# An RWKV layer's chain outputs in two tiles by steps, its inverse issued as one block, and mid products on 64 rows

## The chip, the cores and the metric

One core of a Trainium2 chip runs the whole program. The metric is the device time in microseconds, the median of three runs before. TensorE is PE in the rows, VectorE is DVE, ScalarE is ACT, GpSimd is POOL, SyncE is SP; PEld is TensorE's loading of weights.

## What is computed

Two blocks of a network on a sequence of 512 tokens of width 1024, in float32: attention and an MLP, an RWKV-7 mixer and an MLP, then a second block with a state space model, a linear recurrent unit and a gate. The change is in the RWKV mixer alone. It has 16 heads of 64 and two directions; per direction:

```
def rwkv7_scan(r, w, k, v, kk, a):
    def step(state, inp):
        r_t, w_t, k_t, v_t, kk_t, a_t = inp
        sa = jnp.einsum('bhvk,bhk->bhv', state, -kk_t)
        state = (state * w_t[:, :, None, :] + sa[..., None] * (kk_t * a_t)[:, :, None, :]
                 + v_t[..., None] * k_t[:, :, None, :])
        return state, jnp.einsum('bhvk,bhk->bhv', state, r_t)
...
        o = rwkv7_scan(*ins)
        if d == 1:
            o = jnp.flip(o, axis=1)
        bonus = jnp.sum(rh * kd * r_k.astype(F32), axis=-1, keepdims=True) * vh
        dir_out.append((group_norm(o, gn_w, gn_b) + bonus.reshape(nB, S, D)) * g.astype(F32))
```

The group norm is over the 64 outputs of a head at a token.

## The kernel before

The mixer takes heads in eight pairs (`p` from 0 to 7) and the 512 tokens in eight chunks of 64. In place of a scan over tokens it solves each chunk with small matrices and carries a 64 by 64 state from chunk to chunk. Both directions run at once: step `n` of the chain works on chunk `n` of direction 0 and on chunk `7 - n` of direction 1 (`chunk_of`). Direction 0 and direction 1 (or the two heads of a pair) sit in the two halves of the 128 partitions; `H(i)` is half `i`, `Q(i)` a quarter.

The work of a pair is written as eleven generators, and each is repeated over the pairs (line 1983):

- `values` (line 1526) projects the values once for all pairs; as it ends it frees its pools and opens others (`late`).
- `front` (1558) loads keys and norms them (products with `sel`, then transposes in `head_bcast`, line 1516); `half` (1595), once per direction, makes decays and the scaled keys `bk` and `ar`.
- `scores` (1677) makes for each of four chunk pairs the masked score matrices in a tile `at` and stores their diagonal blocks (`nd_s`). There are nine `at` tiles, so line 1681 lets a chunk pair's scores start only when the chain has freed the one nine before.
- `inverse` (1713) loads the blocks of 16 by 16 into `X` and, by way of `XL`, in transposed form, and inverts them by elimination in 28 VectorE steps; `merge` (1760) loads them back (`yd`), transposes them (`zd`) and puts them together into inverses of chunks, `tt`.
- `early` (1738) makes the values `uv`.
- `mid` (1830) makes for each chunk pair the matrix `m` that takes the state over a chunk, and the rest of `uv`. Its products `ahead` are issued one chunk pair ahead; then come products of `ax` with `tt`, ScalarE's copies into `ta` and `uv`, products of `at` with `ta`, and VectorE's adds into `m`.
- `chain` (1892) runs the eight steps: products of `uv` with `at` (`free`, begun with zeros from `zb` so that the later ones add), of the state `ss` with `m`, ScalarE's four copies into the next state, and two copies of outputs into `o`.
- `post` (1932) squares and sums `o`, takes the power -1/2 on GpSimd, scales, transposes, adds weights and bonus, multiplies by the gate and stores `y_s`.

What sets the order of all this is `weave` (line 37). It runs the generators beside each other. At each `yield` a generator names the engine and the tiles that its next instructions need, or gives a condition that must hold first. `weave` keeps an account of when each engine and tile would be free by its own costs, resumes the generator that could start first, and fixes each engine's order so. A generator that yields less often is issued in longer blocks. Products go into five banks of PSUM (`pm`, the tile `mb`) that are taken in turn, the chain's into three others (`cp`).

The conditions that the change touches are these two:

```
                    yield lambda: done["post"] > p - 1 and late      # line 1894, chain
                    yield lambda: done["step"] >= 8 * p + 8          # line 1949, post
```

With them `o` is one tile, written by eight steps of a pair and then normed as a whole. After the layer's last `post` the output projection loads `y_s` (line 1997) and the rest of the program follows.

Of the kernel before, what the change touches and what calls it, by code (L numbers as in the profile page):

```python
# [13 lines left out]
ALU = mybir.AluOpType  # L14
# [10 lines left out]
class Net:  # L25
# [1279 lines left out]
    def rwkv(self, g_pre, mu_p, mu_n, w_r, w_k, w_v, w_o, k_k, k_a, r_k, gn_w, gn_b, w0, w1, w2, a0, a1, a2,  # L1305
# [64 lines left out]
        with c0:  # L1370
# [86 lines left out]
            with ExitStack() as c1:  # L1457
# [19 lines left out]
                tts, ss, tas = zeros("tt", [8, 2, 64]), zeros("ss", [2, 128]), zeros("ta", [2, 2, 2, 64])  # L1477
                for j, t in enumerate(tts + ss + tas):
                    (V, G)[j % 2].memset(t, 0.0)
# [15 lines left out]
                done["side", 0] = done["side", 1] = 0  # L1495
# [217 lines left out]
                def inverse(p, st):  # L1713

                    yield lambda: done["pre"] > p
                    XL = sh.tile([128, 16, 32], F32, name="XL", tag="v1")
# [9 lines left out]
                    for j in range(1, 15):  # L1726
# [11 lines left out]
                def early(p, st):  # L1738
# [91 lines left out]
                def mid(p, st):  # L1830
# [5 lines left out]
                    def ahead(i):  # L1836
                        b = bank().rearrange("p (j h e x) -> p j h e x", j=2, h=2, e=2)
                        at = st["q", i]
                        for j in range(2):
# [3 lines left out]
                            for hp in range(2):  # L1843
                                for d in range(2):
                                    MM(b[H(d), j, hp, 1, :], at[:, j, hp, 2 * d, H(d)], uv[d][:, cs[d], hp, :], True, True)
                        return b

                    for i in range(4):
# [33 lines left out]
                        for d in range(2):  # L1882
                            cs = slice(6 - 2 * i, 8 - 2 * i) if d else slice(2 * i, 2 * i + 2)
                            r = ar[d][:, cs, 1 - d, :]
                            TT(V, m[:, :, d, H(d)], b[:, :, d, H(d)], r[:, ::-1] if d else r, AD)
                        i4 = lambda t: t.rearrange("p j d x -> p j (d x)")[:, :, 64:192].rearrange("p j (d x) -> p j d x", d=2)
                        TT(V, i4(m), i4(b), ident2.unsqueeze(1).unsqueeze(1).to_broadcast([128, 2, 2, 64]), AD)
# [4 lines left out]
                def chain(p, st):  # L1892

                    yield lambda: done["post"] > p - 1 and late
                    o = late["o"].tile([128, 8, 2, 64], F32, name="o", tag="o")
                    st["o"] = o
# [11 lines left out]
                    for n in range(8):  # L1908
                        if n % 2 == 0:
# [17 lines left out]
                        for d in range(2):  # L1927
                            ACT(o[H(d), chunk_of(n)[d]].rearrange("p h v -> p (h v)"), cp[H(d), d, :], AF.Copy)
# [3 lines left out]
                def post(p, st):  # L1932
# [14 lines left out]
                    yield lambda: done["step"] >= 8 * p + 8  # L1947
                    o = st["o"]
                    o3 = o.rearrange("p c h v -> p (c h) v")
                    rn = stp.tile([128, 16], F32, name="rg", tag="rg")  # L1950
                    for hf in range(2):
                        sq = TQ().rearrange("p (a b) -> p a b", b=64)
                        yield AC, o
                        ACT(sq, o3[:, 8 * hf:8 * hf + 8], AF.Square)
                        yield DV, sq
                        V.tensor_reduce(out=rn[:, 8 * hf:8 * hf + 8], in_=sq, axis=AX.X, op=AD)
                    yield DV, rn
                    TS(V, rn, rn, 1.0 / 64, 64e-5, M, AD)
                    yield PO, rn
# [198 lines left out]
```

## Time and profile before

| | us |
|---|---|
| runs (3): median, lowest, highest | 2320.56, 2318.47, 2324.29 |
| the profiled execution's own time | 2327.65 |
| its span, first to last instruction | 2325.9 |
| TensorE busy in the span | 2139.8 (92%) |
| VectorE, ScalarE, GpSimd busy | 1276.5 (55%), 1084.3 (47%), 91.3 (4%) |
| mean granted TensorE clock | 0.950 of full speed |

The profile page gives the busy time of each engine, forty equal slices of the span, the DMA queues, the chain that ended last and the costliest groups of instructions. The helpers `TT`, `STT`, `ACT` and `MM` record nearly all of the mixer's instructions under lines 1312, 1313, 1315 and 1316, so a row is told apart by the tiles that it names, written as out<-in. A float32 product stands in the trace as two instructions. Busy time counts an instruction from start to its modelled end.

### The profile page before, as it was taken

Reading aid. Unit: us, or ns where it says so; the run is one execution under the profiler, and the core shown is the slowest. Engines: PE = TensorE matmul, PEld = TensorE weight load, DVE = VectorE, ACT = ScalarE, POOL = GpSimd, SP = SyncE. Lnnn points to the kernel's source line nnn. Section 1 sums busy time; section 2 is a strip of 40 time slices with the busy share of each in tenths; the row PEclk is TensorE's granted clock in tenths of the full one; section 3 lists DMA queues with packets and bytes.
Section 4 is the critical chain, followed back from the end, with each engine's and each line's share of the span. In section 5 each row is a group of like instructions: output and inputs, shape, how many; then the busy total and the mean of one; then the engine's idle time right before and its main releaser. Section 6 shows DMA issues by size and latency. Waiting matters only on the chain. (4 is left out here: it accounts for less than half of the span.)

```text
span 2325.9 us, 40409 instructions
## 1 busy us (share of the span) xinstructions
PE 2139.8 (92%) x16330; PEld 1725.7 (74%) x16330; DVE 1276.5 (55%) x2597; ACT 1084.3 (47%) x1982; POOL 91.3 (4%) x123
## 2 busy tenths in 40 slices
PE   8998999999978788888888789999999999999998
PEld 6777788888866566666666568887788877788877
DVE  4656542333488765666764264387645567633353
ACT  4555353332366554777766545333233444522332
POOL 0000000000000001111100000000001000000000
PEclk9999999999989888899999799999999988899999
DMA  5311233233333233222222243334334544233341
GB/s 173 105 55 54 71 95 100 76 114 91 91 103 96 93 102 78 63 57 57 53 55 47 103 127 116 91 91 143 111 112 142 149 120 119 56 94 89 106 145 55
DMA packets 320902, 221.02 MB, mean 95 GB/s; under 512 B 82406, under 2 KB 274442, under 8 KB 320714
## 3 DMA queue, kind: packets, MB, share of 16 engines
q1 hardware_dynamic: 319418, 213.70, 32.3%
q10 hardware_dynamic: 1296, 4.72, 0.6%
q8 instruction: 129, 2.11, 0.4%
q14 instruction: 59, 0.48, 0.1%
HBM read 187.10 MB, written 27.07 MB: 92 GB/s over the span
## 5 line engine op out<-in xcount | busy, mean ns | idle before, releaser
L161 ACT ACTIVATE whi<-raw 128x1024 fp32r<-128x1024 f32 x220 | 231.2, 1053 | 534.8 <-PE mm L234 288.0
L162 DVE TENSOR_TENSOR wlo<-raw,whi 128x1024 fp32r<-128x1024 f32 x220 | 266.3, 1214 | 363.5 <-ACT whi L161 361.3
L233 PE MATMUL mm<-uth,whi 128*128 128x512 f32 (+1 forms) x1088 | 417.0, 384 | 2.0 <-ACT uth L197 2.0
L234 PE MATMUL mm<-utl,whi 128*128 128x512 f32 (+1 forms) x1088 | 409.9, 377 | 2.0 <-DVE utl L198 2.0
L235 PE MATMUL mm<-uth,wlo 128*128 128x512 f32 (+1 forms) x1088 | 409.6, 377 | 0.0
L233 PEld LDWEIGHTS mm<-uth,whi 128*128 128x128 f32 x1088 | 211.8, 195 | 41.0 <-ACT uth L197 3.0
L234 PEld LDWEIGHTS mm<-utl,whi 128*128 128x128 f32 x1088 | 211.3, 194 | 39.6 <-DVE utl L198 2.8
L235 PEld LDWEIGHTS mm<-uth,wlo 128*128 128x128 f32 x1088 | 210.9, 194 | 37.5 <-issue 1.1
L235 PE MATMUL mm<-whi,hl 128*128 128x512 f32 x512 | 200.9, 394 | 0.0
L233 PE MATMUL mm<-whi,hh 128*128 128x512 f32 x512 | 200.8, 395 | 0.0
L234 PE MATMUL mm<-wlo,hh 128*128 128x512 f32 x512 | 200.2, 393 | 0.0
L235 PEld LDWEIGHTS mm<-whi,hl 128*128 128x128 f32 x512 | 96.3, 188 | 22.1 <-issue 0.2
L234 PEld LDWEIGHTS mm<-wlo,hh 128*128 128x128 f32 x512 | 96.3, 188 | 21.6
L233 PEld LDWEIGHTS mm<-whi,hh 128*128 128x128 f32 x512 | 96.3, 188 | 21.4 <-issue 0.4
L233 PE MATMUL mm<-whi,uth 128*128 128x512 f32 x224 | 87.9, 398 | 7.0 <-ACT whi L161 6.4
L235 PE MATMUL mm<-whi,utl 128*128 128x512 f32 x224 | 87.9, 396 | 0.0
L234 PE MATMUL mm<-wlo,uth 128*128 128x512 f32 x224 | 87.3, 394 | 0.0
L1315 ACT ACTIVATE ss<-cp,wc 64x64 f32<-64x64 f32 x224 | 69.5, 310 | 28.9 <-PE cp L1316 24.0
L293 DVE TENSOR_TENSOR acc<-mm,acc 128x512 f32<-128x512 f32 x48 | 33.1, 689 | 69.8 <-PE mm L235 69.8
L234 PE MATMUL mm<-mx,whi 128*128 128x512 f32 x160 | 65.7, 410 | 4.5 <-DVE mx L1303 4.4
L233 PE MATMUL mm<-mx,whi 128*128 128x512 f32 x160 | 62.0, 415 | 6.7 <-ACT mx L1302 5.7
L1313 DVE SCALAR_TENSOR_TENSOR mt<-u_pad,vcol,mt 128x512 f32<-128x512 f32 x96 | 67.0, 752 | 0.9 <-ACT mt L1315 0.8
(561 smaller groups left out, 3989.3 us busy)
## 6 DMA issues: line engine op xcount, KB each, us to landing
raw<-in_mlp_w_dram SPq DMA_DIRECT2D x128, 512.0 KB, 4.1
raw<-in_w_in_dram SPq DMA_DIRECT2D x44, 512.0 KB, 3.9
raw<-in_attn_w_in_dram SPq DMA_DIRECT2D x18, 512.0 KB, 4.9
raw<-in_attn_w_out_dram SPq DMA_DIRECT2D x8, 512.0 KB, 3.7
raw<-in_rk_w_k_dram SPq DMA_DIRECT2D x8, 512.0 KB, 5.5
h_s<-h SPq DMA_DIRECT2D x8, 512.0 KB
raw<-in_rk_w_r_dram SPq DMA_DIRECT2D x8, 512.0 KB
raw<-in_rk_w_v_dram SPq DMA_DIRECT2D x8, 512.0 KB, 4.4
```

The lines of the kernel that those rows point to most:

```text
L161: nc.scalar.activation(out=hi[:, :n], in_=raw[:, :n], func=AF.Copy)
L162: nc.vector.tensor_tensor(out=lo[:, :n], in0=raw[:, :n], in1=hi[:, :n].bitcast(F32), op=ALU.subtract)
L233: mm(out, lhsT=lhs[0], rhs=rhs[0], start=start, stop=False)
L234: mm(out, lhsT=lhs[0], rhs=rhs[1], start=False, stop=False)
L235: mm(out, lhsT=lhs[1], rhs=rhs[0], start=False, stop=stop)
L293: nc.vector.tensor_tensor(out=a, in0=p, in1=a, op=ALU.add)
L1313: STT = lambda e, o, a, s, b, o0, o1: e.scalar_tensor_tensor(out=o, in0=a, scalar=s, in1=b, op0=o0, op1=o1)
L1315: ACT = lambda o, i, f, **k: nc.scalar.activation(out=o, in_=i, func=f, **k)
```

## The change

The outputs of a chain go into two tiles of four steps each, and `post` norms each as soon as its four steps are done; a chain waits, before steps 0 and 4, for the `post` half of the pair before. `inverse` yields no longer between its 28 steps, and `XL` has a tile of its own. In `mid` the products of `at` with `uv` and with `ta` take only the 64 rows that aren't zero, `ta` is written by one copy and no longer kept with zeros, the products with `ta` go into two banks (one per direction), the adds into `m` are four, and `uv` is not zeroed.

```diff
@@ inverse
-                    XL = sh.tile([128, 16, 32], F32, name="XL", tag="v1")
+                    XL = sh.tile([128, 16, 32], F32, name="XL", tag="XL")
...
                         TT(V, t, X[:, 0:j, j].unsqueeze(2).to_broadcast([128, j, n]),
                            X[:, j, j + 1:16].unsqueeze(1).to_broadcast([128, j, n]), M)
-                        yield DV, xt
                         TT(V, X[:, 0:j, j + 1:16], X[:, 0:j, j + 1:16], t, AD)
-                        yield DV, X
@@ early
-                    for d in range(2):
-                        yield PO,
-                        G.memset(uv[d][H(d)], 0.0)
@@ mid
-                                    MM(b[H(d), j, hp, 1, :], at[:, j, hp, 2 * d, H(d)], uv[d][:, cs[d], hp, :], True, True)
+                                    MM(b[H(d), j, hp, 1, :], at[H(1 - d), j, hp, 2 * d, H(d)], uv[d][H(1 - d), cs[d], hp, :], True, True)
...
-                        ta = tas[i % 2]
-                        for d in range(2):
-                            ACT(ta[H(d), d], b[H(d), :, :, 0:64], AF.Copy)
+                        ta = mp.tile([128, 2, 2, 64], F32, name="ta", tag="ta")
+                        ACT(ta, b[:, :, :, 0:64], AF.Copy)
...
-                        b = bank().rearrange("p (j d x) -> p j d x", j=2, d=2)
+
+                        bs = [bank()[:, :256].rearrange("p (j x) -> p j x", j=2) for _ in range(2)]
                         for j in range(2):
-                            for d in range(2):
-                                for hp in range(2):
-                                    MM(b[H(hp), j, d, :], ta[:, d, j, hp, :], lhs(at[:, j], d, hp), True, True)
-                        yield DV, b
+                            for hp in range(2):
+                                for d in range(2):
+                                    MM(bs[d][H(hp), j, :], ta[H(d), j, hp, :], lhs(at[:, j], d, hp)[H(d)], True, True)
@@ chain
-                    yield lambda: done["post"] > p - 1 and late
-                    o = late["o"].tile([128, 8, 2, 64], F32, name="o", tag="o")
+                    yield lambda: late
...
+                        if n % 4 == 0:
+
+                            yield lambda: done["post", n // 4] > p - 1
+                            o = st["o", n // 4] = late["o"].tile([128, 4, 2, 64], F32, name="o", tag=f"o{n // 4}")
...
-                            ACT(o[H(d), chunk_of(n)[d]].rearrange("p h v -> p (h v)"), cp[H(d), d, :], AF.Copy)
+                            ACT(o[H(d), n % 4].rearrange("p h v -> p (h v)"), cp[H(d), d, :], AF.Copy)
@@ post
-                    yield lambda: done["step"] >= 8 * p + 8
...
+                    for half in range(2):
+                        yield lambda: done["step"] >= 8 * p + 4 * half + 4
+                        o = st["o", half]
...
+                        done["post", half] += 1
```

The planner makes another order of it. Three places show how.

ScalarE at the border of two pairs, before: the last copy of outputs (`o<-cp`), and what follows. `tmp<-o` is the squaring in `post`, `ss<-cp` the copies into the state; the next of these is the 28th row of this piece.

```order
L1315 ACTIVATE o<-cp 64x128 x2
L1315 ACTIVATE tmp<-o 128x512
L1315 ACTIVATE tt_6068<-mb 32x8x32 x4
L1315 ACTIVATE uv_10790<-mb 64x4x128 x2
L1315 ACTIVATE tmp<-o 128x512
L1315 ACTIVATE ax<-mb 128x512
L1315 ACTIVATE tmp<-k,vcol_4753 128x512
L1315 ACTIVATE at<-mb 128x2x128 x2
L1315 ACTIVATE tmp<-tmp 128x512
L1315 ACTIVATE ta_6072<-mb 64x256 x2
```

The same border in the change:

```order
L1315 ACTIVATE o<-cp 64x128 x2
L1315 ACTIVATE tmp<-o 128x512
L1315 ACTIVATE uv_10862<-mb 64x4x128 x2
L1315 ACTIVATE ax<-mb 128x512
L1315 ACTIVATE ta<-mb 128x256
L1315 ACTIVATE uv_9959<-mb 64x256
L1315 ACTIVATE uv_9960<-mb 64x2x128
L1315 ACTIVATE ss_6071<-cp,wc 64x64 x4
L1315 ACTIVATE o<-cp 64x128 x2
```

Counted from the last outputs, the next pair's first state copies have moved from the 28th row to the eighth.

VectorE in the inverse of a pair, before: the steps are those with `xt` in them, `o<-o,rg` is the scaling in `post`, `m` the adds of `mid`.

```order
L1312 TENSOR_TENSOR xt__10018<-X 128x56
L1312 TENSOR_TENSOR X<-X,xt__10018 128x7x8
L1312 TENSOR_TENSOR o<-o,rg 128x512
L1314 TENSOR_SCALAR rn<-mb 128x8
L1312 TENSOR_TENSOR xt__10018<-X 128x56
L1314 TENSOR_SCALAR tmp<-tmp 128x8x64
L1312 TENSOR_TENSOR X<-X,xt__10018 128x8x7
L1312 TENSOR_TENSOR m<-mb,ar_8126 128x2x64
L1312 TENSOR_TENSOR m<-mb,ar_8134 128x2x64
L1312 TENSOR_TENSOR m<-mb,ident_6066 128x2x128
```

In the change, the end of the block of 28 and what stands behind it, down to the score masks (`at<-mb,mk`):

```order
L1312 TENSOR_TENSOR X<-X,xt__9140 128x13x2
L1312 TENSOR_TENSOR xt__9140<-X 128x14
L1312 TENSOR_TENSOR X<-X,xt__9140 128x14
L1732 MEMSET X 128x16
L1312 TENSOR_TENSOR bk_9180<-tmp 128x4x64
L1312 TENSOR_TENSOR ar_9075<-tmp 128x4x64
L1312 TENSOR_TENSOR bk_9180<-tmp 128x4x64
L1312 TENSOR_TENSOR ar_9075<-r,tmp 128x4x64
L1664 COPY wc<-tmp 64x8 x2
L1312 TENSOR_TENSOR tmp<-r,tmp 128x512
L1312 TENSOR_TENSOR o<-o,rg 128x512
L1312 TENSOR_TENSOR at<-mb,mk 128x2x2x128 x2
```

Nothing stands between the steps any more; what stood there has moved ahead of the block or behind it.

TensorE early in the section, before: the end of 24 value products (`mb<-mx`), then a key norm's products with `sel`, the transposes of `head_bcast` and the next 48 value products, behind which the first merge stands.

```order
L233 MATMUL mb<-mx,whi 128x512
L234 MATMUL mb<-mx,whi 128x512
L235 MATMUL mb<-mx,wlo 128x512
L1316 MATMUL mb<-sel_4968,tmp 32x2 x16
L1523 MATMUL mb<-ident,tmp 128x128 x4
L233 MATMUL mb<-mx,whi 128x512
```

In the change the products with `sel` stand ahead of the 24:

```order
L1316 MATMUL mb<-lhl,wl 128x512
L1316 MATMUL mb<-cmat,v 128x128 x4
L1316 MATMUL mb<-sel_4968,tmp 32x2 x16
L233 MATMUL mb<-mx,whi 128x512
L234 MATMUL mb<-mx,whi 128x512
L235 MATMUL mb<-mx,wlo 128x512
```

and the transposes come after those 24, followed at once by the first half of the merge:

```order
L233 MATMUL mb<-mx,whi 128x512
L234 MATMUL mb<-mx,whi 128x512
L235 MATMUL mb<-mx,wlo 128x512
L1523 MATMUL mb<-ident,tmp 128x128 x4
L1316 MATMUL mb<-zd,at 32x32 x2
L1316 MATMUL mb<-yd,at 32x32 x2
```

So the `sel` products moved ahead of 24 value products, and the merge's first half ahead of the last 48.

## Rows read from the trace of the kernel before

**Rows 1.** Windows: stretch, length, busy us of PE, PEld, DVE, ACT, POOL; clock, DMA.

```profile
core 0: us, PE busy (x) PEld busy (x) DVE busy (x) ACT busy (x) POOL busy (x), PEclk, DMA share, GB/s
911.50:1325.40 413.90, 355.80 (x7336) 279.51 (x7322) 242.07 (x678) 290.42 (x759) 41.99 (x34) 0.93 0.23 55
1085.00:1103.00 18.00, 15.46 (x301) 12.28 (x288) 14.60 (x45) 14.14 (x28) 4.88 (x4) 0.91 0.26 65
1210.00:1243.00 33.00, 30.37 (x746) 24.09 (x747) 12.79 (x32) 22.66 (x69) 1.89 (x2) 1.00 0.23 49
```

**Rows 2.** Timeline (start, us, engine, line, operation) of ScalarE at two pairs' border.

```profile
1084.72 0.56 ACT L1315 ACTIVATE o<-cp 64x128 f32<-64x128 f32 x2
...
1107.18 1.32 ACT L1315 ACTIVATE ss<-cp,wc 64x64 f32<-64x64 f32 x4
...
1139.19 0.56 ACT L1315 ACTIVATE o<-cp 64x128 f32<-64x128 f32 x2
```

**Rows 3.** Timeline of VectorE: pair 3's last masks, start and end of its inverse.

```profile
1034.40 1.28 DVE L1312 TENSOR_TENSOR at<-mb,mk 128x512 f32<-128x512 f32 x2
...
1038.14 0.39 DVE L1723 COPY X<-XL 64x256 f32<-64x256 f32 x1 [1.79 <-DMA XL<-nd_s]
...
1057.99 0.07 DVE L1734 MEMSET X<- 128x16 f32 x1
```

**Rows 4.** Timeline of VectorE: two steps of an inverse, eleven others between them.

```profile
1092.98 0.24 DVE L1312 TENSOR_TENSOR xt__10018<-X 128x26 f32<-128x26 f32 x1
...
1095.66 0.22 DVE L1312 TENSOR_TENSOR X<-X,xt__10018 128x56 f32<-128x56 f32 x1
```

**Rows 5.** Timeline of TensorE: groups of products of four shapes.

```profile
1082.99 1.21 PE L1316 MATMUL mb<-ar,bk 64*128 64x128 f32 x16
...
1085.59 1.16 PE L1316 MATMUL mb<-cmat,v 128*128 128x128 f32 x8
...
1093.77 1.09 PE L1316 MATMUL mb<-ax,tt 64*64 64x128 f32 x16
...
1097.35 1.09 PE L1316 MATMUL mb<-at,ta 128*64 128x128 f32 x16
```

**Rows 6.** Timeline of TensorE: groups followed by the same and by another shape.

```profile
1287.59 0.69 PE L1316 MATMUL cp<-uv,at 128*64 128x64 f32 x16
...
1288.10 0.39 PE L1316 MATMUL mb<-ident,ar 128*64 128x128 f32 x4
...
1317.61 0.69 PE L1316 MATMUL cp<-uv,at 128*64 128x64 f32 x16
...
1318.22 0.79 PE L1316 MATMUL cp<-ss,m 128*128 128x128 f32 x4
```

**Rows 7.** Timeline of GpSimd, ScalarE and VectorE: a power of 8 columns, and the end.

```profile
1043.42 1.88 POOL L1312 TENSOR_TENSOR rn<-rn,mhalf 128x8 f32<-128x8 f32 x1 [0.78 <-DVE rn L1314]
...
1326.80 0.63 ACT L1315 ACTIVATE tmp<-o 128x512 f32<-128x512 f32 x1 [0.75 <-DVE rg L1956]
...
1328.18 0.17 DVE L1314 TENSOR_SCALAR rg<-rg 128x16 f32<-128x16 f32 x1
...
1328.50 2.90 POOL L1312 TENSOR_TENSOR rg<-rg,mhalf 128x16 f32<-128x16 f32 x1 [30.16 <-DVE rg L1314]
...
1331.43 0.69 DVE L1312 TENSOR_TENSOR o<-o,rg 128x512 f32<-128x512 f32 x1 [3.07 <-POOL rg L1312]
...
1334.18 0.68 DVE L1312 TENSOR_TENSOR o<-o,rg 128x512 f32<-128x512 f32 x1
```

**Rows 8.** Timeline of TensorE and VectorE early in the section.

```profile
887.72 0.43 PE L1316 MATMUL mb<-sel,tmp 128*32 128x2 f32 x32 [1.58 <-ACT tmp L1315]
...
892.60 1.11 PE L1523 MATMUL mb<-ident,tmp 128*128 128x128 f32 x4 [4.45 <-ACT tmp L1315]
...
898.11 0.71 DVE L1770 STREAM_TRANSPOSE zd<-yd 128x512 f32<-128x512 f32 x1
...
906.54 0.22 PE L1316 MATMUL mb<-zd,at 32*32 32x32 f32 x2
```

**Rows 9.** TensorE's waits from 979.5 to 1292.4: total, times, longest.

```profile
PE mb L1316 <- issue: 6.7, 5, 1.8
```

More of the change, by code (lines that the diff above doesn't have):

```diff
@@ L1475, in rwkv @@
                 zeros = lambda nm, shape: [sh.tile([128] + shape, F32, name=f"{nm}{j}") for j in range(2)]
-                tts, ss, tas = zeros("tt", [8, 2, 64]), zeros("ss", [2, 128]), zeros("ta", [2, 2, 2, 64])
-                for j, t in enumerate(tts + ss + tas):
+                tts, ss = zeros("tt", [8, 2, 64]), zeros("ss", [2, 128])
+                for j, t in enumerate(tts + ss):
                     (V, G)[j % 2].memset(t, 0.0)
@@ L1494, in rwkv @@
                 done = dict(values=0, merge=0, lora=0, tail=0, early=0, bk=0, pre=0, inverse=0, mid=0, post=0, step=0)
-                done["side", 0] = done["side", 1] = 0
+                done["side", 0] = done["side", 1] = done["post", 0] = done["post", 1] = 0
                 X, yd, zd = (sh.tile([128, 16, 32], F32, name=n) for n in ("X", "yd", "zd"))
@@ L1946, in post @@
                         ys.append(y)
-                    yield lambda: done["step"] >= 8 * p + 8
[L1948 to L1951, printed above, removed]
+                    for half in range(2):
+                        yield lambda: done["step"] >= 8 * p + 4 * half + 4
+                        o = st["o", half]
+                        o3 = o.rearrange("p c h v -> p (c h) v")
+                        rn = stp.tile([128, 8], F32, name="rg", tag="rg")
                         sq = TQ().rearrange("p (a b) -> p a b", b=64)
                         yield AC, o
-                        ACT(sq, o3[:, 8 * hf:8 * hf + 8], AF.Square)
+                        ACT(sq, o3, AF.Square)
                         yield DV, sq
[L1956 to L1959, printed above, removed]
-                    TT(G, rn, rn, self.mhalf.to_broadcast([128, 16]), ALU.pow)
-                    for half in range(2):
-                        yield DV, rn
-                        TT(V, o3[:, 8 * half:8 * half + 8], o3[:, 8 * half:8 * half + 8], rn[:, 8 * half:8 * half + 8].unsqueeze(2).to_broadcast([128, 8, 64]), M)
+                        V.tensor_reduce(out=rn, in_=sq, axis=AX.X, op=AD)
+                        yield DV, rn
+                        TS(V, rn, rn, 1.0 / 64, 64e-5, M, AD)
+                        yield PO, rn
+                        TT(G, rn, rn, self.mhalf.to_broadcast([128, 8]), ALU.pow)
+                        yield DV, rn
+                        TT(V, o3, o3, rn.unsqueeze(2).to_broadcast([128, 8, 64]), M)
                         yield PE, o
@@ L1966, in post @@
                         for q in range(4):
-                            nc.tensor.transpose(b[:, q, :], o[:, half * 4 + q].rearrange("p h v -> p (h v)"), self.ident)
+                            nc.tensor.transpose(b[:, q, :], o[:, q].rearrange("p h v -> p (h v)"), self.ident)
+                        done["post", half] += 1
                         for d in range(2):
                             yield DV, b
-                            y3 = c64(ys[d])[:, half * 4:half * 4 + 4]
+                            y3 = c64(ys[d])[:, 4 - half * 4:8 - half * 4][:, ::-1] if d else c64(ys[d])[:, half * 4:half * 4 + 4]
                             STT(V, y3, b[:, :, H(d)], col("gw", p), y3, M, AD)
```

7 lines of the change are left out of this document (3 added, 4 removed).

## The prediction

> **What bounds the kernel now.** I read the page's forty slices first, to see where TensorE is not full. Outside the RWKV layer it is full or nearly so; the one long stretch of eights and sevens is the layer's woven section, and the order of TensorE, VectorE and ScalarE outside that section is the same before and after but for names. So only the woven section can change, and every number below comes from it.
>
> Then the windows by stage. From 911.5 us (all values projected, first pair about to be merged) to 1325.4 us (last output of the last chain copied) TensorE is busy 355.80 of 413.90 us, 86%; ScalarE is busy 290.42 and VectorE 242.07 [rows 1]. TensorE has the most work, but 58 us of idle time. The question is what that idle time is made of.
>
> The timeline of ScalarE at one pair's border comes next. Pair 2's chain copies its last output at 1084.72; pair 3's first state copy starts at 1107.18; pair 3's last output at 1139.19 [rows 2]. So a pair takes 54.5 us, and for 22 us of it the chain stands still. Line 1894 says why: a chain may not start before the post part of the pair before it has taken the outputs out of the single tile `o`. In the pause TensorE still has other work (15.46 of 18.00 us busy), while in a stretch where the chain runs it reaches 30.37 of 33.00, or 92% [rows 1].
>
> There is a second loop, two pairs long. Line 1681 lets the scores of a pair be made only as chain steps free their `at` tiles, nine chunk pairs ahead. In VectorE's timeline the last scores of pair 3 are masked at 1034.40, the inverse's first copy starts at 1038.14 and its last instruction at 1057.99, so the inverse takes 20 us [rows 3]; the chain that needs it starts at 1107.18 [rows 2]. The 28 steps need far less: twelve of them that stand close together take from 1092.98 to the end of the last at 1095.88, 0.24 us each [rows 4], so 28 are 6.8 us. The other 13 us are VectorE's other work, let in between.
>
> So the section is held by two dependency loops, with TensorE close behind them.
>
> **The change part by part.**
>
> *Outputs in two halves.* The pause of 22 us goes: the first half is normed and transposed while steps 4 to 7 run, so its tile is free when the next chain's step 0 writes it, and the second half's has four further steps to come free. *Inverse in one block.* 13 us go from a loop of two periods, 109 us, so 6.5 us per pair; VectorE is held for 6.8 us in return, and what it evacuates waits behind it. With both loops shorter than TensorE's own work, TensorE is what is late next: its work divided by the density that it reaches. I take 92%, the densest long stretch of the trace, which is one without a pause [rows 1]; the ends are 86% (the waits stay as they are) and 96%.
>
> *Products on 64 rows.* The 16 instructions of a group at,ta (8 products, two instructions each) take 1.09 us now [rows 5]. In the change they use four positions of the array instead of two, into two banks. At best half is saved, 0.55 us; at worst nothing. Eight products that alternate two row halves with two banks take 1.21 us, while four over all rows take 1.16 [rows 5], so row pairing does work here, though not to the full. I take 0.4 us; with 32 groups that is -12.8 us. Against it: the products uv,at change shape and now alternate with ident,ar, which does not. A group of 16 is followed after 0.51 us by one of the same shape (1287.59 to 1288.10) and after 0.61 by one of another (1317.61 to 1318.22) [rows 6], so a change of shape costs 0.10 us. Three more per call of `ahead`, 32 calls: +9.6 us. Net -3.2 us of TensorE work: 352.6.
>
> 352.6 / 0.92 = 383.3 us in place of 413.9: **-30.6 us**.
>
> *The end.* After the last step one half is left to norm. The second square and sum go (1326.80 to 1328.18, 1.4 us); the power on GpSimd has 8 columns instead of 16 (1.88 for 2.90 us, -1.0); the scaling, transposing and adding of the first half go (1331.43 to 1334.18, 2.7 us) [rows 7]. Together **-5.1 us**, all on the path, as nothing else runs there. Bounds: 4 to 6.
>
> *The fill.* The planner's new order moves one thing for the worse. In an early key norm the products with `sel` now stand 24 value products earlier. In the trace they waited for ScalarE until 887.72, and the 24 products ran meanwhile; now these stand behind them. There they cover the wait of the next transposes (4.45 us before 892.60), but the first merge, which now stands ahead of the last 48 value products, needs VectorE's transpose of 898.11, which ends at 898.8 [rows 8]. In the trace 48 value products lie between the transposes' end, 893.7, and the merge at 906.54, 12.8 us with a slow start; so the values end 11 to 13 us after 898.8, at about 911, 4 to 5 us later than now, with one merge product group (some 1 us) already done. **+3.6 us**; bounds 0 and 6.
>
> *Costed at nothing.* The two ScalarE copies into `ta` become one (32 times); VectorE's three adds into `m` become four; the power runs twice per pair; the memsets of `uv` and `ta` on GpSimd and VectorE go. All lie on engines that stand idle for 30% and more of the section [rows 1]; if ScalarE were the bound, fewer copies would help, not hurt. The inverse's loads keep their place on SyncE's queue behind the same stores, and their own tile takes away a wait that the trace does not show. One more bank per `mid` step is taken out of five that turn; that is a cost that I cannot price but in the density.
>
> Sum: -30.6 - 5.1 + 3.6 = -32.1 us. The profiled execution took 2327.65 us, so it would take 2295.5; it stands 7.1 us over the median of the runs, 2320.56, and so I forecast **2288 us** for the median. Its own range, with densities of 88% and 96%, is 2272 to 2306. A measurement of this kernel can tell about 0.3%, 7 us, from no change.
>
> **The rivals.**
>
> *The pause was full.* TensorE was 86% busy in the pause, and 86% over the section [rows 1]: the waits may be those of an order planned with wrong durations, and not of the loops. Then density stays at 86%: 352.6 / 0.86 = 410.0, -3.9; with the end and the fill -5.4: 2315 us. For it: TensorE's waits are many and short; the costliest kind between the first and the seventh chain's end comes to 6.7 us in five times [rows 9]. Against it: 92% where the chain runs beside much other work. Chance 0.17.
>
> *Denser still.* If four positions save the full half and density goes to 96%, 347.8 / 0.96 = 362.3, -51.6, with the end and the fill -53: 2267 us. Chance 0.13.
>
> *Two row halves into one bank.* The new uv,at products come from two row halves and land in one bank. If they ran one after the other there, each call of `ahead` would pay for its 8 products once more, at most the 0.69 us that 16 such instructions take [rows 6]: 32 times, 22 us, 24 at a density of 92%: 2312 us. The trace speaks against it: ax,tt are such products (two row halves, one bank) and take the same 1.09 us as at,ta, which are not [rows 5]. The rule is the Trainium skill's, that different row tiles cannot access the same PSUM bank at a time (TensorEngine Tiling (Array Packing), section Gotcha 1: PSUM Pressure); the trace, with 1.09 us for both, does not bear it out for tiles in different columns. Chance 0.05.
>
> *The block stops TensorE.* For 6.8 us per pair VectorE takes nothing out of PSUM: score masks, chain matrices, bonus sums queue behind it, five banks turn, and TensorE stops until the block is over. Eight blocks wholly exposed cost 54 us, against 32 gained: 2342 us. It decides when TensorE loses over 5 us per block ((32 + 7) / 8). For it: behind the block there stand, in the new order, eight more instructions before the next score masks. Against it: in the trace VectorE was held in short steps for 20 us and TensorE was 86% busy, and ScalarE can go on evacuating. Chance 0.06.
>
> **How the numbers follow.** The forecast has 0.59, the rivals 0.17, 0.13, 0.05 and 0.06. The range 2268 to 2314 takes in the forecast's bounds, most of the full pause and the one bank, and the upper part of the denser case; it leaves out the block and some of each end, under 0.2. Faster by over 7 us (below 2313.6): nearly all of the forecast, the denser case, half of the full pause and of the one bank, 0.81. Slower: 0.07. The rest, 0.12, is within 0.3%.
>
> **What would show it.** Right: in ScalarE's timeline the last output copy of a pair and the first state copy of the next lie under 8 us apart; the inverse takes about 7 us from first to last instruction; the period of a pair is 48 to 50 us; TensorE is over 90% busy between the first and the last chain; at,ta takes about 0.7 us per 16 instructions; some 10 us lie between the last output copy and the store of `y_s`. Wrong: a period above 52 us with the pause gone (the full pause); TensorE's waits on VectorE's masks growing from a few us to tens (the block); uv,at twice as long (one bank).

## The result and the profile after

The changed kernel takes 2354.82 us (median of 4 runs, 2348.12 to 2360.13); the kernel before, on the same chip, 2321.36. The ratio is 1.0148, with a 95% interval of 1.0126 to 1.0171. The forecast was 2288 us with a range to 2314: the sign is wrong. What came is the rival that was given 0.06, the block that stops TensorE, which had 2342 us. The profiled executions lie 25.6 us apart (2327.65 and 2353.24 us), the medians 33.5, as the one of before stands 7 us above its median.

The windows of the changed kernel, columns as in [rows 1]; the first stretch is the same one, from 911.5 us to the last output of the last chain:

```profile
911.50:1357.09 445.59, 374.91 (x7484) 282.68 (x7483) 254.31 (x722) 277.60 (x731) 34.72 (x30) 0.87 0.21 49
1171.00:1178.30 7.30, 7.30 (x99) 5.62 (x92) 6.42 (x30) 1.36 (x5) 1.70 (x2) 0.69 0.01 2
1178.30:1182.80 4.50, 0.39 (x3) 0.14 (x2) 4.32 (x16) 2.13 (x6) 0.11 (x1) 0.94 0.20 62
1182.80:1190.00 7.20, 7.19 (x76) 5.27 (x76) 3.96 (x10) 4.69 (x11) 0.00 (x0) 0.50 0.37 64
```

The stretch grew from 413.90 to 445.59 us [rows 1], by more than the two executions differ: all of the loss lies here. It does not hold quite the same work, though: at 911.5 us the change still projects values (its last value product starts at 914.71 us, that of before at 906.22). From a place at which TensorE's order is still the same in both kernels to the last output copy, before and then the change:

```profile
879.19:1325.38 446.19, 382.09 (x7707) 300.38 (x7706) 258.29 (x723) 303.23 (x780) 45.46 (x37) 0.93 0.24 57
878.45:1357.08 478.63, 397.80 (x7711) 300.89 (x7710) 269.19 (x765) 288.42 (x748) 36.35 (x31) 0.86 0.21 50
```

On this equal work TensorE's busy time rose by 15.7 us, as the granted clock fell from 0.93 to 0.86, and the time in which it is not busy from 64.1 to 80.8 us. So the 32.4 us are about 16 of clock and 17 of standing still.

The other three windows show one place where that happens. VectorE's timeline there, then TensorE's, then ScalarE's (start, us, engine, line, operation; the idle time before and its releaser in brackets):

```profile
1165.39 0.29 DVE L1312 TENSOR_TENSOR m<-mb,ar 128x128 f32<-128x128 f32 x1 [6.32 <-PE mb L1316]
...
1172.01 0.38 DVE L1723 COPY X<-XL 64x256 f32<-64x256 f32 x1
...
1172.69 0.17 DVE L1312 TENSOR_TENSOR xt__10922<-X 128x14 f32<-128x14 f32 x1
...
1179.05 0.18 DVE L1312 TENSOR_TENSOR X<-X,xt__10922 128x14 f32<-128x14 f32 x1
...
1181.47 0.68 DVE L1312 TENSOR_TENSOR o<-o,rg 128x512 f32<-128x512 f32 x1
1182.08 1.28 DVE L1312 TENSOR_TENSOR at<-mb,mk 128x512 f32<-128x512 f32 x2
```

```profile
1164.68 0.66 PE L1316 MATMUL mb<-at,ta 64*64 64x128 f32 x15
...
1170.46 0.61 PE L1316 MATMUL mb<-selr,tmp 128*32 128x2 f32 x32 [4.03 <-DVE tmp L1312]
1171.00 1.12 PE L1316 MATMUL cp<-uv,at 128*64 128x64 f32 x16
1172.06 2.08 PE L1316 MATMUL mb<-ar,bk 64*128 64x128 f32 x16
...
1178.26 0.43 PE L1316 MATMUL mb<-at,ta 64*64 64x128 f32 x2
1182.81 1.12 PE L1316 MATMUL mb<-at,ta 64*64 64x128 f32 x14 [4.13 <-DVE at L1312]
```

```profile
1176.89 0.38 ACT L1315 ACTIVATE ta<-mb 128x256 f32<-128x256 f32 x1 [8.61 <-PE mb L1316]
```

The scores (ar,bk) are in PSUM by 1174.1, but their mask on VectorE runs only at 1182.08: the block, from 1172.69 to 1179.2, and eight more instructions stand ahead of it. TensorE gets two of the sixteen at,ta instructions out (one product of eight); the next product takes the second bank, and it starts 4.13 us later, as the mask is written. That it waits for the bank, and not for data, no row says; the run with a sixth bank below bears it out. TensorE then works at 0.50 of its clock, 1.2 GHz, for the 7 us that follow, in which 14 instructions of at,ta take 1.12 us; ahead of the stall 15 took 0.66. A stall is paid twice, once as idle time and once as half speed after it: the scores of 1172.06, behind a stall of 4.03 us, take 2.08 us instead of 1.21 [rows 5]. (That stall, ahead of the block, is not the block's: the bonus sums of `selr` wait there for a product that stands behind VectorE's scalings of keys. It comes back below.) ScalarE meanwhile waits 8.61 us for TensorE, so the chain does not move either.

TensorE's waits from 980 to 1290 (total, times, longest):

```profile
PE mb L1316 <- DVE at L1312: 21.4, 5, 6.1
PE mb L1316 <- DVE tmp L1312: 8.6, 3, 4.0
```

In the trace of before, the largest kind came to 6.7 us [rows 9] and the wait on VectorE's masks to 6.0:

```profile
PE mb L1316 <- DVE at L1312: 6.0, 6, 1.7
```

ScalarE at three borders of pairs, the last output copy and the first state copy of the next chain; then the end of the section:

```profile
1043.46 0.56 ACT L1315 ACTIVATE o<-cp 64x128 f32<-64x128 f32 x2
...
1055.65 1.27 ACT L1315 ACTIVATE ss<-cp,wc 64x64 f32<-64x64 f32 x4
...
1102.57 0.56 ACT L1315 ACTIVATE o<-cp 64x128 f32<-64x128 f32 x2
...
1120.20 1.29 ACT L1315 ACTIVATE ss<-cp,wc 64x64 f32<-64x64 f32 x4
...
1165.21 0.56 ACT L1315 ACTIVATE o<-cp 64x128 f32<-64x128 f32 x2
...
1177.95 1.28 ACT L1315 ACTIVATE ss<-cp,wc 64x64 f32<-64x64 f32 x4
```

```profile
1356.53 0.56 ACT L1315 ACTIVATE o<-cp 64x128 f32<-64x128 f32 x2
```

```profile
1368.23 0.36 SPq L1977 DMA_DIRECT2D y_s<-tmp  x1
```

The chain's pause of 22 us [rows 2] became 12 to 18 us (2.5 and 1.9 us at the last two, which are not shown; under 8 was forecast for all), and yet the period of a pair is 59 and 63 us where it was 54.5: what the pause gave, the chain's own steps lost.

### The profile page after: what moved, and what is told of

It reads as the page before. It is cut to its first block, busy times and chain, and to the rows that moved or that the text cites. A ratio compares the mean times of both kernels' runs of the same rounds, so it can differ in the third digit from the quotient of the medians.

```text
span 2351.4 us, 40418 instructions
## 1 busy us (share of the span) xinstructions
PE 2142.5 (91%) x16330; PEld 1715.8 (73%) x16330; DVE 1285.0 (55%) x2636; ACT 1069.1 (45%) x1950; POOL 78.6 (3%) x114
## 4 chain that ended last, share of the span: by engine, by line
PE 76%; DVE 11%; ACT 7%; DMA 3%; issue 2%; POOL 0%; SPq 0%; ACTq 0%; DVEq 0%; POOLq 0%
PE mm L233 19%; PE mm L234 19%; PE mm L235 19%; PE mb L1316 7%; PE cp L1316 3%; ACT tmp L1315 2%; DVE mt L1313 1%; PE pv L605 1%; DVE wlo L162 1%; ACT ss L1315 1%; PE ptr L1099 1%; PE ptr L590 1%; PE mm L563 1%; DVE X L1312 1%; PE mb L233 1%
```

## The experiments

In all sets the kernel before took between 2318.5 and 2321.4 us, so medians of different sets are compared to within 3 us, besides the interval of each ratio, which is 3 to 8 us to either side. The unit of the argument is the same stretch, from 911.5 us to the last output copy; a window is one execution, which can lie some us off its median.

### The parts: no block, 64 rows alone, 64 rows with the block, six banks

No block is the change with the inverse's yields put back:

```diff
                         TT(V, t, X[:, 0:j, j]..., M)
+                        yield DV, xt
                         TT(V, X[:, 0:j, j + 1:16], X[:, 0:j, j + 1:16], t, AD)
+                        yield DV, X
```

> The change with the two yields put back into the inverse, so that its 28 steps are planned one by one again; the outputs in two halves and the products on 64 rows stay. If the block is what holds TensorE up (VectorE empties no bank for some 7 us, with the keys' products on both sides of it), this is about 2290 us, below the kernel before, and TensorE's waits on VectorE's masks fall from 21 us to under 8. If the two halves spoil the planner's order, it stays at 2340 to 2355. If the products on 64 rows with their second bank are the cause, it stays at 2340 or above too.

Measured: 2314.52 us, ratio 0.9978 (0.9964 to 0.9993). Without the block the change is 5 us faster than before in the same set (2319.84), not 30 as expected, and the waits on the masks are gone (0.8 us in 2). Its window, and the one of equal work:

```profile
911.50:1312.92 401.42, 355.27 (x7310) 266.83 (x7309) 246.91 (x721) 276.32 (x727) 33.74 (x30) 0.91 0.23 53
877.23:1312.91 435.68, 382.91 (x7711) 288.98 (x7710) 263.74 (x767) 289.02 (x748) 35.38 (x31) 0.90 0.23 55
```

Against the change, with the same instructions on TensorE in the second, 43.0 us: 14.9 of busy time (the clock) and 28.1 of idle time.

64 rows alone is the kernel before with `mid` and `early` of the change:

> The kernel before with the products on 64 rows alone (one output tile, post as a whole, the inverse step by step, its own XL tile). If these products only save the TensorE time that they save in the change (0.4 us in each of 32 groups, against 0.1 us for each change of shape), this is 2310 to 2322 us. If the second bank per step or the changes of shape are the cause of the loss, it is 2340 or above.

Measured: 2334.56 us, 1.0064 (1.0039 to 1.009): **15 us slower** than before, where the forecast had -3. (`XL` kept its old tag here.) With the block on top:

> The kernel before with the products on 64 rows and the inverse in one block, but with one output tile and post as a whole. If the block is the cause of the loss by itself, this is 30 us or more over the run with the products on 64 rows alone. If the block hurts only together with the halves, the two are within 10 us of each other.

Measured: 2372.73 us, 1.0222 (1.019 to 1.0255). So the block costs 38 us here (with `XL`'s own tile, which it brings along) and 40 with the halves, and the halves give 18 to 20 on either. The sixth bank, on the change itself in its own order:

```diff
-pm, pu = P1("pm", 5, space=PSUM), P1("pu", 3, space=PSUM)
+pm, pu = P1("pm", 6, space=PSUM), P1("pu", 2, space=PSUM)
```

> The change, instruction for instruction in the same order, but with six banks in turn for all products and two for the chain's in place of five and three. If TensorE loses its time because the bank that it needs next still waits for VectorE behind the block, a sixth bank takes away a good part of the 21 us of waits on masks and this is 2335 us or less. If it waits for data and not for banks, or if the chain's third bank matters more, it stays at 2350 or rises.

Measured: 2341.58 us, 1.0094 (1.0068 to 1.012). One more bank takes back 13 of the 40 us, between the two expectations, so part of the cost is indeed TensorE without a bank. But the stalls stay. All sixteen at,ta instructions now pass, and the next group that takes a bank waits for the mask in their place:

```profile
1176.51 1.11 PE L1706 MATMUL mb<-ident,bk 128*128 128x128 f32 x4 [4.48 <-DVE at L1312]
```

```profile
PE mb L1706 <- DVE at L1312: 14.5, 3, 5.5
PE mb L1316 <- DVE at L1312: 5.5, 1, 5.5
```

The waits on the masks (980 to 1290) are 20.0 us in sum where they were 21.4: one bank more moves a stall of this length by one group and does not bridge it. The stretch was run at a clock of 0.90 in place of 0.87; how the bank brings that about is not shown. The Trainium skill asks for a turn of banks (Perfetto Trace Analysis, section Optimizing Tensor Performance): independent products should rotate through them, so that one is emptied while the next is filled. The runs agree as far as the 13 us for the sixth go.

### The block: order or piece?

With the block, the planner orders everything else anew. To part the two, the planner's picks among its eleven generators were written down, and a kernel followed them word for word in place of the rule of least start:

```diff
-            x = min(go, key=lambda x: ...)
+            x = next(y for y in live if y[4] == RWKV_ORDER[len(picks)])
```

TensorE, ScalarE and GpSimd then get the section's instructions in the order written down, whatever is done with the 28 steps.

> The change, with the order in which its generators were taken written down and followed word for word, so that TensorE and ScalarE get every instruction of these pairs in the same order as in the change; only the inverse's 28 steps no longer stand in one piece, one of them follows each of the next 28 picks, and the merge's first pick (DMAs only) comes behind the last of them. Theory 'held' (VectorE is taken for 7 us, the evictions behind the block come late, TensorE stops and its clock falls): the cost of the block goes, 2308 to 2322, as with the two yields back. Theory 'order' (the planner, which sees one lump, puts the other engines' work in a worse order, and that is what costs): it stays, 2345 to 2360. A mixture would stand between.

Measured: 2357.96 us, 1.0174 (1.0151 to 1.0196): no gain at all. The inverse took 9.9 us here from its first copy (1117.31) to its last memset (1127.16), against 7.2 for the block of 1172.01, so VectorE was loaded almost as densely; as most picks are other engines', 8 to 22 steps still stand together in each inverse, for up to 5.2 us.

> The change in its own order, followed word for word, with the inverse's 28 steps left out (the triangular inverse isn't formed, everything else is). Theory 'held': VectorE is free for 7 us more per pair and the inverse's result comes 7 us sooner; 2285 to 2312, at or under the kernel with the two yields back (2314.5). Theory 'order': TensorE's order is the change's, so 2335 to 2355.

Measured: 2321.79 us, 1.0007 (0.9991 to 1.0023), between the two theories. The reverse, one block in the order of the kernel without it:

> The change's block, but every engine but VectorE gets its work in the order of the kernel with the two yields back (that order written down and followed): the 28 steps stand in one piece where that kernel has the first of them, all else in its place. Theory 'order' (not the piece of 7 us costs, but what the planner makes of the rest of the program around it): as that kernel, 2310 to 2322, and PE's waits on DVE near its 9.5 us. Theory 'held' (the piece itself stops TensorE, whatever the order): 2340 to 2355, with waits on DVE of 30 us and more.

Measured: 2338.26 us, 1.0072 (1.0051 to 1.0092). The window and the waits on VectorE from 980 to 1290:

```profile
911.50:1334.90 423.40, 363.06 (x7264) 270.13 (x7263) 252.06 (x720) 277.24 (x727) 33.79 (x30) 0.88 0.21 50
```

```profile
PE mb L1343 <- DVE tmp L1339: 8.2, 2, 4.5
PE mb L1989 <- DVE rn L1341: 5.9, 1, 5.9
PE mb L1989 <- DVE o L1339: 4.5, 1, 4.5
```

So the piece of 7 us by itself costs 24 us, here by the post part's transposes and the `selr` products that wait for VectorE. The same order without the steps:

> The same order as in the run with the block in it, with the 28 steps left out (the triangular inverse isn't formed). It says what the steps cost at all in a good order: theory 'order' expects little, 2300 to 2314, so that leaving out the steps is worth under 15 us here against 33 us in the change's order. Theory 'VectorE's load decides in any order': about 33 us less than the kernel with the two yields back, 2278 to 2288.

Measured: 2312.2 us, 0.9966 (0.995 to 0.9982):

```profile
911.50:1304.44 392.94, 350.13 (x7264) 263.03 (x7262) 214.57 (x524) 277.12 (x727) 33.68 (x30) 0.91 0.23 54
```

In this order the 28 steps, laid out singly, are worth 2 us in the median, within what can be told: they are hidden. (The two windows differ by 8.5 us; the profiled execution with the steps lay 3 us above its median, this one 4 below.) Next, the block in four pieces, planned anew:

```diff
                         TT(V, X[:, 0:j, j + 1:16], X[:, 0:j, j + 1:16], t, AD)
+                        if j % 4 == 3:
+                            yield DV, X
```

> The change with the block cut in four pieces of 6, 8, 8 and 6 steps (a yield behind each, and the planner free to order again); a piece is 1.5 to 2 us. Theory 'held', with its 5 us below which nothing is late: as with the yields at every step, 2310 to 2318. Theory 'order', where the planner takes other streams against a lump of any size: a part of the cost stays, 2322 to 2340.

Measured: 2355.47 us, 1.0142 (1.0118 to 1.0166), as slow as one block and above both expectations, though an inverse now takes up to 17 and 19 us (1096.89 to 1114.14, 1160.86 to 1179.95; others 9 to 11). Its window and its largest wait:

```profile
911.50:1349.74 438.24, 373.96 (x7473) 281.12 (x7471) 252.35 (x724) 279.47 (x731) 34.30 (x30) 0.87 0.21 50
```

```profile
PE mb L1316 <- DVE tmp L1312: 16.6, 5, 4.8
```

The 5 us of the rival were no length below which a piece is harmless, as this expectation has it, but the loss per block at which the sum turns. Nor did the pieces stay apart: a piece of 8 steps takes 1.93 us, but in six of the eight inverses two of them stand together, 14 or 16 steps in 3.2 to 3.9 us. Length alone does not decide, either: in the kernel before, 13 steps or more stand together for 3.1 us or more in six of the eight (twelve such steps in [rows 4]). Two more runs in this order:

> Every engine's work in the order of the kernel with four pieces, followed word for word, with the 28 steps left out (the triangular inverse isn't formed). Theory 'order': what the planner makes of the other work costs most, 2335 to 2350. Theory 'the pieces': without them the order is as good as another, 2310 to 2325 (the change's own order without the steps took 2321.8, the good one 2312.2).

Measured: 2327.43 us, 1.0036 (1.0019 to 1.0053). Its largest wait on VectorE is still there without a single step of the inverse:

```profile
PE mb L1343 <- DVE tmp L1339: 15.4, 5, 4.0
```

> The order of the kernel with four pieces, followed word for word, with the steps of each piece laid out singly, one behind each of the following picks. Theory 'order': no gain, 2345 to 2358. Theory 'the pieces': 2315 to 2330.

Measured: 2349.09 us, 1.0141 (1.0097 to 1.0184). The nine together, in us:

| order that the planner made for | no steps | steps singly | in pieces or one piece |
|---|---|---|---|
| single steps | 2312.2 | 2314.5 | 2338.3 (one) |
| four pieces | 2327.4 | 2349.1 | 2355.5 (four) |
| one block | 2321.8 | 2358.0 | 2354.8 (one) |

Read down the first column: the orders that the planner makes around lumps are worse by 15 us (four pieces) and 10 us (one block) with no inverse in them at all. Read across: in the good order the steps cost 2 us singly and 26 in a piece; in the other two they cost 22 to 36 in any form. There VectorE has no slack where they stand, and laying them out over the next few picks does not make any. So both theories hold a part. How the 40 us divide depends on the way through the table: by the block's order without steps, 10 of order and then 33 of steps (2 of which are paid in the good order too); by the good order with the block, 24 of the piece and then 17 of order.

TensorE's waits from 980 to 1290 tell the two parts apart. In the change's order without the steps, and below it in the good order without them:

```profile
PE mb L1343 <- DVE tmp L1339: 8.6, 3, 4.0
PE mb L1343 <- DVE at L1339: 1.0, 3, 0.6
```

```profile
PE mb L1343 <- DVE tmp L1339: 3.7, 1, 3.7
```

The waits on the masks, 21.4 us in the change, are gone without the steps: they are the block's. The waits on `tmp`, those of the `selr` products behind VectorE's scalings of keys, are 8.6 us with and without the steps, 15.4 in the order of four pieces and 3.7 in the good one: they are the order's. Why the planner puts those products there is not settled.

### The block alone

The kernel before with the block. `XL` kept its old tag here too, so it is the block and nothing else, against what the expectation says of the tile:

> The kernel before with the 28 steps issued as one block, and nothing else (XL in a tile of its own, as in the change). Theory 'effects add' (the block costs the same 38 us with or without the halves): 2350 to 2362. Theory 'it takes the second bank for the block to cost so much': 2325 to 2340.

Measured: 2380.83 us, 1.0241 (1.0206 to 1.0277): 59 us, more than with the change's other parts and above both ranges. The block needs neither the second bank nor the halves to cost what it does. But it stops TensorE elsewhere: the waits on masks are 3.9 us, and the largest on VectorE is that of the post part's transposes, whose scaling of `o` stands behind the block:

```profile
PE mb L1965 <- DVE o L1312: 12.4, 5, 4.9
```

With one output tile the chain waits for that too: its pause between pairs is 27 to 35 us at the first five borders (before: 18 to 23). What `XL`'s old tile adds to the 59 us was not run.

### Why do the 64-row products cost 15 us?

First on the change without its block: the uv,at products on 128 rows again, with their memsets, and at,ta still on 64 (no change of shape left in `ahead`); a sixth bank; and both.

```diff
-MM(..., at[H(1 - d), j, hp, 2 * d, H(d)], uv[d][H(1 - d), cs[d], hp, :], True, True)
+MM(..., at[:, j, hp, 2 * d, H(d)], uv[d][:, cs[d], hp, :], True, True)
```

> The change with the inverse's two yields back and the uv,at products as before, on 128 rows with the zeroed halves of uv (16 more memsets on GpSimd); the at,ta products stay on 64 rows. Theory 'shape changes' (the switch between 64 and 128 rows, estimated at 0.10 us, 96 of them in the eight pairs): 9 to 10 us less on TensorE, 2303 to 2308. Theory 'not on the path or not the switches': 2312 to 2318.

Measured: 2310.45 us, 0.9958 (0.9944 to 0.9973), 4 us less than the same kernel with 64 rows. TensorE's busy time shows more:

```profile
911.50:1308.04 396.54, 344.29 (x7310) 269.58 (x7309) 247.01 (x721) 275.77 (x727) 45.10 (x42) 0.91 0.23 54
```

344.29 against 355.27 us at a clock that reads 0.91 in both: 11 us, give or take the 4 us that one hundredth of the clock is worth. Call by call it can be read more closely, below.

> The change with the inverse's two yields back, and six PSUM banks for the products and two for the chain (five and three before). Theory 'the 64-row products' second bank is what costs': the sixth bank gives it back, 2298 to 2307. Theory 'banks only buffer TensorE while VectorE is held': without the block nothing to buffer, 2311 to 2318.

Measured: 2312.36 us, 0.9963 (0.9944 to 0.9982): 2 us, within what can be told. Without the block the bank alone hardly matters.

> The change with the two yields back, the uv,at products on 128 rows and six PSUM banks for products: the parts that helped, together. Theory 'effects add' (-4 of the 128 rows, -2 of the sixth bank): 2306 to 2311. Theory 'both take the same stalls': 2309 to 2314.

Measured: **2303.24 us, 0.9914 (0.989 to 0.9938)**, faster than both kernels, and below both expectations: on top of the 128 rows the sixth bank gave 7 us, not 2:

```profile
911.50:1300.91 389.41, 339.38 (x7310) 266.92 (x7309) 245.90 (x721) 276.95 (x727) 45.15 (x42) 0.92 0.24 55
```

The period of one pair is 50.5 us in it (first state copies at 1088.90 and 1139.44), though the chain still stands still for 18 us between pairs (1070.56 to 1088.90). That pair is not all: by the last output copies, its first five periods are 47 to 56 us, those of before 50 to 55.

Then on the kernel before, against the 2334.56 of 64 rows:

> The kernel before with the at,ta products on 64 rows in two banks, ta in one copy, and the uv,at products left on 128 rows with their memsets. Theory 'switches' (of the 15 us that the 64 rows cost, 11 are the shape changes, as TensorE's busy time in the runs without the block says): 2318 to 2325. Theory 'order or banks': 2329 to 2335, at most 4 us less than with both on 64 rows.

Measured: 2317.7 us, 0.9983 (0.9965 to 1.0001).

> The kernel before with both products on 64 rows, and six PSUM banks for the products and two for the chain. Theory 'banks' (the mid step takes one more of five): 2318 to 2325. Theory 'order' or 'switches': 2329 to 2335, since a sixth bank gave 2 us to the kernel with halves and no block.

Measured: 2319.18 us, 0.9988 (0.9969 to 1.0006).

> The kernel before with both products on 64 rows, where every engine gets its work in the order of the kernel before (written down and followed; the second bank's m sums stand right behind the first's). Theory 'order': the cost goes, 2314 to 2322. Theory 'the products themselves' (bank, switches): 2329 to 2337.

Measured: 2327.71 us, 1.0038 (1.0017 to 1.0058). The windows of 64 rows, and of 64 rows for at,ta alone:

```profile
911.50:1331.27 419.77, 368.36 (x7332) 273.30 (x7320) 243.65 (x710) 275.46 (x727) 29.66 (x22) 0.89 0.22 51
```

```profile
911.50:1311.88 400.38, 345.96 (x7287) 269.44 (x7276) 242.41 (x709) 274.74 (x726) 41.62 (x34) 0.91 0.23 53
```

Without the shape changes 17 us come back, with the sixth bank 15, with the old order 7. These do not add up to 15: each of the first two gives back the whole cost, the third about half. What 64 rows did in the stretch is not more standing still (51.4 us, against 58.1 before) but a lower clock (0.89 against 0.93) and a longer busy time. That the place is tight in three ways at once would fit; no run shows how a bank and a change of shape lead to the same 15 us.

## Why the prediction was wrong

**The bound.** Its first step read two loops of waiting and held TensorE's own work to be a limit 14% away. The loops are real but were not what set the pace: the pause fell to 12 to 18 us and the time rose; and the best kernel has a pair of 50.5 us, near the 48 to 50 of the forecast, with a pause of 18. A pause of the chain is not lost time while TensorE works through it, and [rows 1] said that it did (15.46 of 18.00 us).

**The density.** This is the step that failed: "352.6 / 0.92", with no term for the block beside it. A density was carried over from a stretch of 33 us in which VectorE is busy 12.79 us [rows 1], to a section in which the change puts VectorE's work into lumps. In the change TensorE is busy 84% of the stretch, not 92%, and at a clock of 0.87, which the division by a density leaves out: it took the busy time as fixed, and that grew by 16 us on equal work. Nor did it come without the block: there TensorE is busy 88.5% at a clock of 0.91 (355.27 of 401.42 us), and 87% in the best kernel. The time without the block, 2314.52 us, is the one that the rival of the full pause had (2315, for a density that stays at 86%); that its mechanism is the same is not shown. (The forecast's range took 88% as its low end where the text says 86%.) The change's own cost, 40 us as measured, was in the text ("VectorE is held for 6.8 us in return, and what it evacuates waits behind it") but not in the sum.

**The block as a rival.** Its mechanism and its place were right (masks late, banks full, TensorE stopped: 21.4 us of waits on the masks where there were 6.0), though banks are a part of it alone (13 us for a sixth). Its price of 54 us lies between the 40 in the change and the 59 of the block alone; 2342 us came out too low because the 32 us gained did not come. Its chance of 0.06 was too low. The argument against it, that VectorE had been held in short steps for 20 us and TensorE was 86% busy, does not hold: steps that the planner could lay in gaps cost nothing that can be told (2 us for all 224), a block cost 24 to 59 us. Its line of 5 us per block rested on the 32 us gained: the blocks lost 5.0 us each (40 / 8), but the rest of the change had gained 5 us in all.

**The inverse's gain.** "6.5 us per pair" from a loop of two periods: the inverse did fall to 7 us (1172.01 to 1179.2), as expected; nothing came of it. Its length was not the bound: with the steps left out altogether, the good order gained 2 us.

**The products on 64 rows.** The saving was sized right, 0.67 us per 16 of at,ta where 0.7 was forecast; the price was not. One call of `ahead`, from its first instruction to the next group's, before and then in the change, both at full clock:

```profile
1242.31 0.44 PE L1316 MATMUL mb<-ident,ar 128*64 128x128 f32 x4
1242.58 0.40 PE L1316 MATMUL mb<-uv,at 128*64 128x64 f32 x8
...
1243.36 1.16 PE L1316 MATMUL mb<-cmat,v 128*128 128x128 f32 x8
```

```profile
1159.16 0.44 PE L1316 MATMUL mb<-ident,ar 128*64 128x128 f32 x4
...
1160.65 0.71 PE L1316 MATMUL cp<-ss,m 128*128 128x128 f32 x4
```

1.49 us in place of 1.05, 0.44 more and not 0.30. The changes of shape are three more, as forecast, but each costs 0.15 us: in the trace's single instructions the next start comes 0.10 us later, and the second pair of products 0.05 later again. 32 calls are 14.1 us against 13.4 saved (32 times 0.42), so the net of -3.2 us was nothing. What was missed beyond that is that it came out as +15 us on the kernel before, through the clock (0.93 to 0.89) and the tighter turn of banks that was "a cost that I cannot price".

**The halves.** 18 to 20 us for the better, in both comparisons; the forecast had put its 30.6 and 5.1 us on them, the inverse and the rows together. **The end** is 11.7 us from the last output copy to the store of `y_s` (before: 15.3, from 1324.83 to 1340.17), 3.6 us gained where 5.1 was forecast, just under its bounds of 4 to 6. **The fill** was read in the right direction and too small: the last value product starts 8.5 us later (914.71 for 906.22), where 4 to 5 were forecast; without the block it starts at 903.10. What this cost no run parts from the rest.

**Two row halves into one bank** did not come. Eight instructions, four of the new products, pass in 0.45 us (TensorE's timeline of the change, with a group of at,ta below):

```profile
1052.68 0.45 PE L1316 MATMUL mb<-uv,at 64*64 64x64 f32 x8
...
1218.08 0.67 PE L1316 MATMUL mb<-at,ta 64*64 64x128 f32 x16
```

Eight of 128 rows take 0.40 us (1242.58), and the 0.05 is that of the change of shape; after it the products of the two row halves start in pairs, one pair 0.05 us behind the other, as those of 128 rows do. So nothing runs twice. By the Trainium skill (TensorEngine Tiling (Array Packing), section Gotcha 1: PSUM Pressure) different row tiles cannot access one bank at a time; the measurement does not show a price for it here. The same page (section Tiling Modes) says that a change of tiling mode drains TensorE; the trace agrees as far as the 0.15 us for each change go.

## What to carry to other kernels

An engine that is busy 55% of the time can still be the one that everybody waits for: work put on it in one piece can cost up to its length (3 to 7 us for each block of 6.5 us here) where other engines' buffers turn through it, and the place to look is not its busy share but what stands behind the piece in its queue, and how many buffers bridge it. When a stall is priced, add what the clock takes after it: half of the loss in this stretch. And where a planner sets the order, an edit of the work is also a new order, worth 10 to 15 us here; follow the old order word for word to see the one without the other.

## What was not expected of the hardware

A busier TensorE had the lower clock: 88% of the stretch busy at 0.89 with 64-row products (368.36 of 419.77 us), 86% at 0.93 before [rows 1]. The lower clock itself makes the share larger: busy time times clock, as an estimate of the work at full clock, is 328 and 331 us. So the busy share of a long stretch does not tell the clock; behind the stalls of 4 us above it went to 1.2 GHz, though the engine was then busy without a gap. And four tiles of 64 by 64 took 0.67 us for what two of 128 by 64 did in 1.09 [rows 5], not half. Within the group they gain the full half: in the trace's single instructions a round of four starts every 0.09 us (1218.24, 1218.35, 1218.46), a round of two every 0.10 before; what is left over is the first round (0.16 us to the second) and the end.
